# A gating unit's small product, issued three ticks instead of two behind the scaling of its rows

## The chip, the core and the metric

The kernel runs on one core of a Trainium2 chip. The metric is the device time of one execution in microseconds (us), the median of several runs. Lower is better.

The engines named here: PE (matmul; PEld is its weight load), DVE (vector), ACT (scalar, activations), POOL (GpSimd, which also issues some transfers), SP (which issues most transfers). Each works through its own queue in order and waits for others by semaphores.

## The reference, cut to what matters

One decoder layer on 512 tokens of width 2048, in float32. Of it, this case touches the spatial gating unit (gMLP):

```python
proj  = rmsnorm(x, attn_norm_g) @ w_in           # [u | v_sgu | q | k | v_att | g_a | g_b]
u     = gelu(u)
v_sgu = rmsnorm(gelu(v_sgu), sgu_norm_g)         # over each group of 128 columns
...
mixed = einsum('gts,bnsgc->bntgc', tril(w_s), v) # chunks of 128 tokens, 8 groups
y_a   = u * (mixed + b_s)
```

The rest (stick-breaking attention, two gated up-projections, w_o, SwiGLU, a gated per-layer embedding) only matters as the work that stands around it.

## The kernel before

All activations lie transposed: columns on the 128 partitions, the 512 tokens along a row. A large product is done over 256-column **units** by a seven-product (Strassen) scheme, each operand split into a high and a low part (`whi`, `wlo`) so that three fp32r matmuls stand for one fp32 matmul. For one output block of 256 columns a **Pair** runs through 8 inner units, taken two by two: four **doubles**, each with its own slot of split weights (three slots in rotation: `whi_75/wlo_76`, `whi_77/wlo_78`, `whi_79/wlo_80`). `L701` is the matmul of the five products whose right operands stand doubled, `L296` to `L298` are the three matmuls of the other two.

Weights of a double come in by two SP transfers (`L341`, `L349`) into a landing; then POOL issues a transfer that adds two further blocks onto them (`L370`); ACT makes the high parts (`L366`, five blocks, then two), DVE two more sums (`L382`) and the low parts (`L363`). ACT copies finished PSUM products out (`L757`) and DVE combines them (`L760`) during the last double of a block.

**Ticks.** While `Pair.add` writes out a double it calls `tick()` twice: after the fourth and after the seventh product, so a block of four doubles holds eight ticks. Work that stands beside the large products is written as generators; `beside(steps)` starts one a tick later, and each `yield n` asks to be continued n ticks on. So a `yield` is a place in every engine's program, not a time. The order of the PE program is the order of writing; the other engines' small instructions are placed by the framework's scheduler, with the weights' own instructions chained in their order.

**The gating unit.** The output blocks run `... s0 s1 u0 s2 u1 s3 u2 u3 ...`. A block `s` holds two groups. When it is done, DVE scales it by the row norm (`L1250`), ACT applies gelu (`L1344`; `L1348` for a `u`), and `sgu_v` starts beside the next blocks. For each of its two groups ("first half", "second half"): SP fetches the group's spatial weights (`L1222`, then masked by POOL, `L1223`) and biases (`L1226`); two ticks later PE flips the rows (`L1055`, four transposes into a bank of the two-bank pool `small`), ACT takes the squares (`L1062`, four times), DVE scales them (`L1231`), POOL raises them to -1/2 (`L954`, called the pow below); a tick later ACT scales the flipped rows (`times`, four `L1078`); some ticks later PE multiplies them with the spatial weights (`L1240`, four fp32 matmuls, each of which reads one of the four quarters that `L1078` wrote), and DVE scales the product and adds the bias (`L1241`). Then the second half begins in the same step. At `L1349` a `u` block is multiplied into the result. s0's second half and s1's first half overlap; s2 and s3 stand alone.

Both halves share one tile for the spatial weights and one for the bias, so the next `L1222` waits for `L1240`, and the next `L1226` for `L1241`.

Of the kernel before, what the change touches and what calls it, by code (L numbers as in the profile page):

```python
# [70 lines left out]
def hybrid_layer(  # L71
# [109 lines left out]
    def small_bank():  # L181
        return psa.tile([P, T], F32, tag="small", name=nm("small"))
# [769 lines left out]
    def power(ms, n):  # L952
        r = rms_tile()[:, :n]
        nc.gpsimd.tensor_tensor(out=r, in0=ms, in1=expo[:, :n], op=ALU.pow)  # L954
        return r
# [89 lines left out]
    def a_tile(tag, n=T, start=0):  # L1045
        return att[tag].f(start, start + n)
# [4 lines left out]
    def flip(o):  # L1051

        ps = small_bank()
        for t in range(NT):
            nc.tensor.transpose(ps[:, t * P : (t + 1) * P], o[:, t * P : (t + 1) * P], ident)  # L1055
        return ps

    def squares(ps):

        ms, junk = small(NT), tmp.tile([P, P], F32, tag="diag", name=nm("sq"))  # L1060
        for t in range(NT):
            nc.scalar.activation(junk, ps[:, t * P : (t + 1) * P], AF.Square,  # L1062
                                 accum_out=ms[:, t : t + 1])
        return ms
# [10 lines left out]
    def times(dst, ps, r):  # L1075
        for t in range(NT):
            s = slice(t * P, (t + 1) * P)
            nc.scalar.activation(dst[:, s], ps[:, s], AF.Copy, scale=r[:, t : t + 1])  # L1078
# [138 lines left out]
    def sgu_v(rnd, o):  # L1217

        for h in range(2):
            g = 2 * rnd + h  # L1220
            ws = a_tile("w2", P, rnd % 2 * P)
            nc.sync.dma_start(out=ws, in_=wsT[g])  # L1222
            nc.gpsimd.affine_select(out=ws, in_=ws, pattern=[[1, P]], compare_op=ALU.is_ge,  # L1223
                                    fill=0.0, base=0, channel_multiplier=-1)
            bb = a_tile("w1", P, rnd % 2 * P)
            nc.sync.dma_start(out=bb, in_=b_s[g : g + 1, :].broadcast_to([P, P]))  # L1226
            yield 2
            gv = a_tile(("l", "w0")[rnd % 2])
            ps = flip(o[:, h * T : (h + 1) * T])
            ssq = squares(ps)  # L1230
            nc.vector.tensor_scalar(out=ssq, in0=ssq, scalar1=1.0 / P, scalar2=EPS,  # L1231
                                    op0=ALU.mult, op1=ALU.add)
            rr = power(ssq, NT)
            yield 1
            times(gv, ps, rr)
            yield 2
            mp = small_bank()
            for t in range(NT):
                s = slice(t * P, (t + 1) * P)
                nc.tensor.matmul(mp[:, s], gv[:, s], ws, start=True, stop=True)  # L1240
            nc.vector.scalar_tensor_tensor(  # L1241
                out=o[:, h * T : (h + 1) * T].rearrange("p (n t) -> p n t", t=P),
                in0=mp.rearrange("p (n t) -> p n t", t=P),
                scalar=gcol[:, g_sgu + g : g_sgu + g + 1],
                in1=bb.unsqueeze(1).to_broadcast([P, NT, P]),
                op0=ALU.mult, op1=ALU.add)
# [78 lines left out]
    for n, ((w, i), pr) in enumerate(zip(order, made())):  # L1325
        if n == 0:
            row1 = norm1.row()
            for eps, c in ((eps_cols, EPS), (eps_q, EPS * P)):
                nc.vector.tensor_scalar(out=eps, in0=norm1.mean, scalar1=c, scalar2=None,
                                        op0=ALU.mult)  # L1330
        if n == 0:
            a_tiles()
        o = pr.out(block(w, i) if n < 3 else None)
        if w == "q":
            beside(q_prep(o, i))
        elif w == "k":
            kT, rk = o, rms_tile()
            beside(k_prep(kT, rk))
            beside(attention(i, kT, rk, a_tile("v", 1024)), 6)
        elif w == "v":  # L1340
            beside(v_prep(o, a_tile("v", 1024)))
        elif w == "s":
            scaled(o, row1)
            nc.scalar.activation(o, o, AF.Gelu_apprx_tanh)  # L1344
            beside(sgu_v(i, o))
        elif w == "u":
            scaled(o, row1)
            nc.scalar.activation(o, o, AF.Gelu_apprx_tanh)  # L1348
            nc.vector.tensor_tensor(out=y_a[i].f(), in0=o, in1=y_a[i].f(), op=ALU.mult)  # L1349
            y_done["a", i] = True  # L1350
        else:
            d = tc.dram_tile([P, 1024], F32, name=nm("gsp"))
            nc.sync.dma_start(out=d, in_=o)
            gate_spill[w, i] = d
# [250 lines left out]
```

## Time and profile before

| | |
|---|---|
| median of 3 runs | 2653.82 us (2651.19 to 2657.2) |
| the profiled execution's own time | 2652.22 us |
| its span | 2650.5 us |
| outside the span (difference) | 1.72 us |
| instructions | 42355 |
| stretch in which the gating unit runs | about 620 to 765 us |
| DVE busy over the span | 2255.1 us (85%) |
| ACT busy over the span | 1409.0 us (53%) |
| POOL busy over the span | 451.5 us (17%) |
| mean DMA rate | 212 GB/s |

The views used: the page's shares by engine; the waits (who waited for whom, total in us, times, longest); the chain of work that ended last, in order of time (start, duration, what); the busy time of each engine by stretch; and the timeline of single engines (start, duration, instruction, and in brackets the idle time before it and what released it). PE's instruction times are partly modelled and those of POOL are rough.

### The profile page before, as it was taken

Reading aid. Unit: us, or ns where it says so; the run is one execution under the profiler, and the core shown is the slowest. Engines: PE = TensorE matmul, PEld = TensorE weight load, DVE = VectorE, ACT = ScalarE, POOL = GpSimd, SP = SyncE. Lnnn points to the kernel's source line nnn. Section 1 sums busy time; section 2 is a strip of 40 time slices with the busy share of each in tenths; the row PEclk is TensorE's granted clock in tenths of the full one; section 3 lists DMA queues with packets and bytes.
Section 4 is the critical chain, followed back from the end, with each engine's and each line's share of the span. In section 5 each row is a group of like instructions: output and inputs, shape, how many; then the busy total and the mean of one; then the engine's idle time right before and its main releaser. Section 6 shows DMA issues by size and latency. Waiting matters only on the chain.

```text
span 2650.5 us, 42355 instructions
## 1 busy us (share of the span) xinstructions
PE 2635.0 (99%) x15202; PEld 2301.7 (87%) x15202; DVE 2255.1 (85%) x3856; ACT 1409.0 (53%) x2245; POOL 451.5 (17%) x559
## 2 busy tenths in 40 slices
PE   9999999999999999999999999999999999999999
PEld 7888888889998888888888888888888888889888
DVE  8687878787887558999888888888889989989898
ACT  7756565655554335466444444444445445455543
POOL 0222223232220001101111111111110211211010
PEclk9999999999999999999999999999999999999999
DMA  6777777677775669988888788888887989988794
GB/s 209 183 195 171 194 172 192 171 192 191 175 195 186 223 224 271 254 246 212 223 213 217 197 203 203 195 212 201 202 203 225 255 227 275 225 242 254 239 269 137
DMA packets 288130, 561.46 MB, mean 212 GB/s; under 512 B 26288, under 2 KB 133552, under 8 KB 287920
## 3 DMA queue, kind: packets, MB, share of 16 engines
q1 hardware_dynamic: 225856, 440.77, 50.6%
q0 software_dynamic: 61776, 117.47, 27.8%
q8 instruction: 119, 1.95, 0.3%
q14 instruction: 91, 0.75, 0.1%
q10 hardware_dynamic: 288, 0.52, 0.1%
HBM read 507.28 MB, written 51.38 MB: 211 GB/s over the span
## 4 chain that ended last, share of the span: by engine, by line
PE 94%; DVE 3%; ACT 1%; DMA 1%; issue 1%; SPq 0%; DVEq 0%; ACTq 0%
PE ps L701 56%; PE ps L298 9%; PE ps L297 9%; PE ps L296 9%; PE small L701 6%; DVE wlo L363 1%; PE small L1181 1%; PE small L1129 1%; PE small L1055 1%; DVE parts L287 1%; DVE wholes L534 0%; DVE wholes L382 0%; PE small L1240 0%; DMA wholes<-x 0%; DMA wholes<-w_ffn_out 0%
## 5 line engine op out<-in xcount | busy, mean ns | idle before, releaser
L701 PE MATMUL ps<-parts,whi 128*128 128x512 f32 x4390 | 1470.6, 398 | 1.9 <-DVE out L806 0.8
L366 ACT ACTIVATE whi<-wholes 128x512 fp32r<-128x512 f32 (+2 forms) x934 | 873.1, 948 | 759.4 <-DVE wholes L382 308.6
L363 DVE TENSOR_TENSOR wlo<-wholes,whi 128x512 fp32r<-128x512 f32 (+2 forms) x934 | 980.8, 1086 | 78.5 <-ACT whi L366 77.6
L701 PEld LDWEIGHTS ps<-parts,wlo 128*128 128x128 f32 x4390 | 823.9, 188 | 188.0 <-DVE wlo L363 2.5
L701 PE MATMUL ps<-parts,wlo 128*128 128x256 f32 x4390 | 868.4, 279 | 1.1 <-DVE wlo L363 1.1
L701 PEld LDWEIGHTS ps<-parts,whi 128*128 128x128 f32 x4390 | 707.2, 189 | 11.3 <-issue 3.1
L297 PE MATMUL ps<-parts,whi 128*128 128x256 f32 (+1 forms) x1622 | 538.4, 332 | 1.0 <-DVE parts L287 0.9
L298 PE MATMUL ps<-parts,wlo 128*128 128x256 f32 (+1 forms) x1622 | 538.3, 333 | 1.1 <-DVE wlo L363 1.1
L296 PE MATMUL ps<-parts,whi 128*128 128x256 f32 (+1 forms) x1612 | 532.5, 332 | 1.8 <-ACT parts L286 1.4
L382 DVE TENSOR_TENSOR wholes<-wholes 128x256 f32<-128x256 f32 x820 | 346.3, 422 | 15.8 <-DVE wlo L363 0.4
L760 DVE TENSOR_TENSOR out<-out,ps 128x256 f32<-128x256 f32 x525 | 216.8, 416 | 152.2 <-ACT out L757 152.0
L297 PEld LDWEIGHTS ps<-parts,whi 128*128 128x128 f32 x1622 | 305.9, 189 | 37.9 <-DVE parts L287 2.9
L298 PEld LDWEIGHTS ps<-parts,wlo 128*128 128x128 f32 x1622 | 306.2, 189 | 30.6 <-DVE wlo L363 1.5
L296 PEld LDWEIGHTS ps<-parts,whi 128*128 128x128 f32 x1612 | 303.5, 189 | 32.2 <-ACT parts L286 2.2
L370 POOL DMA_DIRECT2D wholes<-w_ffn_in x169 | 147.6, 873 | 704.2 <-DVE wholes L382 209.7
L370 POOL DMA_DIRECT2D wholes<-w_in x132 | 117.0, 888 | 543.1 <-DMA wholes<-w_in 112.3
L701 PE MATMUL small<-parts,whi 128*128 128x512 f32 x480 | 190.2, 397 | 0.0
L757 ACT ACTIVATE out<-ps 128x256 f32<-128x256 f32 x279 | 104.7, 385 | 57.0 <-PE ps L701 52.9
L287 DVE TENSOR_TENSOR parts<-wholes,parts 128x1024 fp32r<-128x1024 f32 (+3 forms) x139 | 124.0, 904 | 12.6 <-ACT parts L286 12.5
L286 ACT ACTIVATE parts<-wholes 128x1024 fp32r<-128x1024 f32 (+3 forms) x139 | 107.8, 797 | 46.5 <-DVE wholes L534 32.4
L370 POOL DMA_DIRECT2D wholes<-w_ffn_out x64 | 55.9, 873 | 356.0 <-DMA wholes<-w_ffn_out 84.7
L1428 ACT ACTIVATE out<-out 128x512 f32<-128x512 f32 x44 | 27.9, 633 | 156.2 <-DVE out L1427 156.2
(135 smaller groups left out, 1833.6 us busy)
## 6 DMA issues: line engine op xcount, KB each, us to landing
wholes<-w_ffn_in SPq DMA_DIRECT2D x169, 384.0 KB, 5.6
wholes<-w_in SPq DMA_DIRECT2D x132, 384.0 KB, 5.0
wholes<-w_ffn_in SPq DMA_DIRECT2D x169, 256.0 KB, 4.8
wholes<-w_ffn_in POOLq DMA_DIRECT2D x169, 256.0 KB, 5.4
wholes<-w_in SPq DMA_DIRECT2D x132, 256.0 KB, 4.1
wholes<-w_in POOLq DMA_DIRECT2D x132, 256.0 KB, 5.0
wholes<-w_ffn_out SPq DMA_DIRECT2D x64, 384.0 KB, 6.0
wholes<-x SPq DMA_DIRECT2D x46, 512.0 KB, 6.1
```

The source lines that it names most:

```text
L286: return (nc.scalar.activation(hi, src, AF.Copy), nc.vector.tensor_tensor(out=lo, in0=src, in1=hi.bitcast(F32), op=ALU.subtract))
L287: nc.vector.tensor_tensor(out=lo, in0=src, in1=hi.bitcast(F32), op=ALU.subtract))
L296: nc.tensor.matmul(ps, sh, mh, start=start, stop=False)
L297: nc.tensor.matmul(ps, sh, ml, start=False, stop=False)
L298: return nc.tensor.matmul(ps, sl, mh, start=False, stop=stop)
L363: in_turn(nc.vector.tensor_tensor(out=self.lo[:, blocks], in0=r, in1=h.bitcast(F32), op=ALU.subtract))
L366: in_turn(nc.scalar.activation(h, r, AF.Copy))
L370: nc.gpsimd.dma_start(out=raw[:, 3:5], in_=self.src[:, 1:3], accum_op=ALU.add)
L382: in_turn(nc.vector.tensor_tensor(out=o, in0=x, in1=y, op=ALU.add))
L701: m = nc.tensor.matmul(out, l, r, start=first and k == 0, stop=last and k == 1)
L757: in_turn(nc.scalar.activation(out, x, AF.Copy, scale=scale))
L760: in_turn(nc.vector.tensor_tensor(out=out, in0=x, in1=y, op=op))
```

## The change

One number. After the step that issues the scaling of the flipped rows, `sgu_v` lets three ticks go by before it issues the product, where it let two go by:

```diff
             rr = power(ssq, NT)
             yield 1
             times(gv, ps, rr)
-            yield 2
+            yield 3
             mp = small_bank()
             for t in range(NT):
                 s = slice(t * P, (t + 1) * P)
```

No instruction is added or removed. What follows in the generator moves with it: in the first half the product by one tick, and with it the second half's two transfers, mask, flip, squares, pow and scaling; the second half's product by two ticks. The scheduler places the instructions of ACT, DVE, POOL and SP anew around that.

On PE, at the first half of s0, one piece of the difference (`small` is the product's bank, the `ps` are the large product's banks; the block is s1, at the border between its third and fourth double):

```order
@@ -3173,5 +3173,4 @@
 L297 MATMUL ps_6410<-parts,whi_77 128x256
 L298 MATMUL ps_6410<-parts,wlo_78 128x256
-L1240 MATMUL small_6523<-wholes 128x128 x4
 L701 MATMUL ps_6376<-parts,whi_75 128x512
 L701 MATMUL ps_6376<-parts,wlo_76 128x256 x2
@@ -3186,4 +3185,5 @@
 L701 MATMUL ps_6397<-parts,wlo_76 128x256 x2
 L701 MATMUL ps_6397<-parts,whi_75 128x512
+L1240 MATMUL small_6559<-wholes 128x128 x4
 L701 MATMUL ps_6405<-parts,whi_75 128x512
 L701 MATMUL ps_6405<-parts,wlo_76 128x256 x2
```

The four matmuls stood between two doubles and now stand four products into the next one.

On ACT, at the second half of s2, before (the gelu `L1348` is that of u1; `sq`, `ms` are the squares, `rr` the pow's result):

```order
L366 ACTIVATE whi_75<-wholes 128x1280
L1062 ACTIVATE sq_7266,ms_7265<-small_7260 128x128 x4
L1348 ACTIVATE out_7206<-out_7206 128x1024
L366 ACTIVATE whi_75<-wholes 128x512
L366 ACTIVATE whi_79<-wholes 128x1280
L1078 ACTIVATE wholes<-small_7260,rr_7272 128x128 x4
L366 ACTIVATE whi_79<-wholes 128x512
L366 ACTIVATE whi_77<-wholes 128x1280
```

The same place now:

```order
L366 ACTIVATE whi_75<-wholes 128x1280
L1348 ACTIVATE out_7197<-out_7197 128x1024
L366 ACTIVATE whi_75<-wholes 128x512
L366 ACTIVATE whi_79<-wholes 128x1280
L1062 ACTIVATE sq_7298,ms_7297<-small_7292 128x128 x4
L366 ACTIVATE whi_79<-wholes 128x512
L366 ACTIVATE whi_77<-wholes 128x1280
L1078 ACTIVATE wholes<-small_7292,rr_7304 128x128 x4
L366 ACTIVATE whi_77<-wholes 128x512
```

The squares moved behind the gelu and two weight splits, and between them and the scaling stand two weight splits, no longer the gelu and two.

On POOL, from the first half of s1 to that of s2, before (`rr_6701` is the pow of s1's first half, `rr_6842` that of its second, `rr_7131` that of s2's first):

```order
L954 TENSOR_TENSOR rr_6701<-ms_6694,expo 128x4
L370 DMA wholes<-w_in 128x512 x2
L1223 AFFINE_SELECT wholes<-wholes 128x128
L370 DMA wholes<-w_in 128x512
L954 TENSOR_TENSOR rr_6842<-ms_6835,expo 128x4
L370 DMA wholes<-w_in 128x512
L1223 AFFINE_SELECT wholes<-wholes 128x128
L370 DMA wholes<-w_in 128x512 x4
L954 TENSOR_TENSOR rr_7131<-ms_7124,expo 128x4
```

The same place now (`rr_6695`, `rr_6874`, `rr_7131`):

```order
L954 TENSOR_TENSOR rr_6695<-ms_6688,expo 128x4
L370 DMA wholes<-w_in 128x512
L1223 AFFINE_SELECT wholes<-wholes 128x128 x2
L370 DMA wholes<-w_in 128x512 x2
L954 TENSOR_TENSOR rr_6874<-ms_6867,expo 128x4
L370 DMA wholes<-w_in 128x512 x2
L1223 AFFINE_SELECT wholes<-wholes 128x128
L370 DMA wholes<-w_in 128x512 x2
L954 TENSOR_TENSOR rr_7131<-ms_7124,expo 128x4
```

The second half's pow moved behind one more weight transfer. It is the same in s2 and s3.

## The prediction

> **What bounds the kernel now.** First the page: the shares by engine, and the chain that ended last.
>
> ```profile
> PE 2635.0 (99%) x15202; PEld 2301.7 (87%) x15202; DVE 2255.1 (85%) x3856; ACT 1409.0 (53%) x2245; POOL 451.5 (17%) x559
> PE 94%; DVE 3%; ACT 1%; DMA 1%; issue 1%; SPq 0%; DVEq 0%; ACTq 0%
> ```
>
> PE bounds the kernel; all its idle time is 2650.5 - 2635.0 = 15.5 us. The question is how much of that lies where the gating unit runs. The busy time by stretch says none (PE is the first pair after the length), and the weight load's waits between 600 and 800 us are a single line:
>
> ```profile
> 670.00:690.00 20.00, 20.00 (x133) 18.19 (x132) 17.39 (x28) 10.13 (x17) 5.68 (x6) 1.00 0.78 187
> PEld small L1240 <- ACT wholes L1078: 0.2, 1, 0.2
> ```
>
> A busy PE can hide a wait in a matmul's modelled length, so I read the chain's pieces too (start, duration; the first five from s1's second half, the last two from s3's):
>
> ```profile
> 664.83 0.43 PE small L1055 x4
> ...
> 670.20 2.81 PE ps L701 x16
> 673.01 0.89 PE small L1240 x8
> ...
> 676.03 3.50 PE ps L701 x20
> ...
> 718.19 3.50 PE ps L701 x20
> ...
> 757.37 1.18 PE small L1240 x8
> ...
> 760.68 3.50 PE ps L701 x20
> ```
>
> A product costs PE 0.89 us, in the middle of a double as here or between two, and once 1.18: 0.29 us of waiting inside the row. With the 0.2 above, the waits that this edit can remove come to about **0.5 us**, 0.02% of the time. A measurement here can tell about 0.2% (5.3 us) from no change; the three runs shown differ by 6.0 us. So a gain that can be seen is excluded, and the question is what new wait there is.
>
> **How tight the product was.** ACT and POOL at the same place:
>
> ```profile
> 669.30 1.06 ACT L1348 ACTIVATE out<-out 128x1024 f32<-128x1024 f32 x1 [2.42 <-DVE out L1250]
> 670.26 1.78 ACT L366 ACTIVATE whi<-wholes 128x512 fp32r<-128x512 f32 x2
> 671.95 1.14 ACT L1078 ACTIVATE wholes<-small,rr 128x128 f32<-128x128 f32 x4
> ...
> 675.23 1.28 ACT L366 ACTIVATE whi<-wholes 128x1280 fp32r<-128x1280 f32 x1 [0.97 <-PE ps L297]
> ...
> 756.87 1.15 ACT L1078 ACTIVATE wholes<-small,rr 128x128 f32<-128x128 f32 x4 [0.47 <-POOL rr L954]
> ...
> 669.57 0.89 POOL L370 DMA_DIRECT2D wholes<-w_in  x1 [5.05 <-DVE out L1250]
> 670.16 1.74 POOL L954 TENSOR_TENSOR rr<-ms,expo 128x4 f32<-128x4 f32 x1
> 675.74 0.92 POOL L370 DMA_DIRECT2D wholes<-w_in  x1 [3.83 <-DVE wlo L363]
> ...
> 717.82 0.95 POOL L370 DMA_DIRECT2D wholes<-w_in  x1 [3.76 <-DVE wlo L363]
> ```
>
> The scaling `L1078` ends at 673.09 while PE begins the product at 673.01: quarter by quarter, just in time, because it stands on ACT behind the gelu and two splits. PE is not held further because each matmul needs one quarter only. So the two ticks were tight, and a third looks like slack. But the squares, the pow and the scaling of each second half move too, one tick.
>
> **PE's new positions.** A product placed four products into the next double comes, in s1's second half, at 676.03 + 2.81 - 0.89 = 677.95 (its own 0.89 no longer lies ahead of it). In s2's: 718.19 + 2.81 - 0.89 = 720.11. In s3's: 760.68 + 2.81 - 1.18 = 762.31.
>
> **The three second halves: when is the scaling ready?** The squares now stand behind the gelu and two splits, from about 671.9, and take 4 x 0.40 = 1.6 us: 673.5. The 0.40 is the distance of two of them:
>
> ```profile
> 665.30 0.28 ACT L1062 ACTIVATE sq<-small 128x128 f32<-128x128 f32 x1
> ...
> 665.70 0.28 ACT L1062 ACTIVATE sq<-small 128x128 f32<-128x128 f32 x1
> ```
>
> DVE's `L1231` stands behind two `L382` that end about then; no loss. The pow is not next, though: POOL now has the `L370` of 675.74 ahead of it, whose weights SP requested at 671.07, 4.67 us before:
>
> ```profile
> 664.45 0.38 SPq L341 DMA_DIRECT2D wholes<-w_in  x1
> ...
> 671.07 0.38 SPq L341 DMA_DIRECT2D wholes<-w_in  x1
> ...
> 698.44 0.38 SPq L341 DMA_DIRECT2D wholes<-w_in  x1
> ...
> 704.21 0.88 POOL L370 DMA_DIRECT2D wholes<-w_in  x1 [3.33 <-DVE out L760]
> ```
>
> That request is released by DVE and hardly moves, so the pow can start 0.6 us behind the `L370` (670.16 - 669.57), at 676.3. How long it then takes depends on DVE:
>
> ```profile
> 653.95 1.03 POOL L954 TENSOR_TENSOR rr<-ms,expo 128x4 f32<-128x4 f32 x1
> ...
> 697.25 2.06 POOL L954 TENSOR_TENSOR rr<-ms,expo 128x4 f32<-128x4 f32 x1
> ...
> 738.44 0.89 POOL L370 DMA_DIRECT2D wholes<-w_in  x1 [4.57 <-DVE ms L1231]
> 739.00 2.43 POOL L954 TENSOR_TENSOR rr<-ms,expo 128x4 f32<-128x4 f32 x1
> ...
> 669.52 2.09 DVE L363 TENSOR_TENSOR wlo<-wholes,whi 128x1280 fp32r<-128x1280 f32 x2
> ...
> 696.92 2.09 DVE L363 TENSOR_TENSOR wlo<-wholes,whi 128x1280 fp32r<-128x1280 f32 x2
> ...
> 739.08 2.09 DVE L363 TENSOR_TENSOR wlo<-wholes,whi 128x1280 fp32r<-128x1280 f32 x2
> ```
>
> It took 1.03 us with DVE quiet. Beside a pair of low-part splits it ended 0.29 us (671.90 to 671.61), 0.30 us (699.31 to 699.01) and 0.26 us (741.43 to 741.17) behind the pair's end, wherever it had begun. In the new order DVE has, at that time:
>
> ```profile
> 632.18 1.49 DVE L363 TENSOR_TENSOR wlo<-wholes,whi 128x1280 fp32r<-128x1280 f32 x1 [0.43 <-ACT whi L366]
> ...
> 675.46 0.74 DVE L1241 SCALAR_TENSOR_TENSOR wholes<-small,gcol,wholes 128x512 f32<-128x512 f32 x1
> 676.12 0.87 DVE L382 TENSOR_TENSOR wholes<-wholes 128x256 f32<-128x256 f32 x2
> 676.91 2.18 DVE L363 TENSOR_TENSOR wlo<-wholes,whi 128x1280 fp32r<-128x1280 f32 x2
> ...
> 719.07 2.08 DVE L363 TENSOR_TENSOR wlo<-wholes,whi 128x1280 fp32r<-128x1280 f32 x2
> ...
> 761.27 2.09 DVE L363 TENSOR_TENSOR wlo<-wholes,whi 128x1280 fp32r<-128x1280 f32 x2
> ```
>
> `L1241` leaves this place (676.12 - 675.46 = 0.66 us) and `L1231` adds about 0.1, so the split of 676.91 begins at 676.35. Only its first part, 1.49 us, follows at once: the second needs an ACT split that now stands behind the scaling. DVE falls idle at 677.85, and by the rows above the pow ends 0.3 behind, at 678.15. `L1078` follows 0.05 later (671.95 behind a pow that ended at 671.90), and PE can begin about 0.50 after that (757.37 behind 756.87, where it came just in time). So 678.70 against 677.95: **PE waits about 0.75 us.** In s2, with the same step of 0.56 earlier: 719.07 - 0.56 + 1.49 + 0.30 + 0.05 + 0.50 = 720.85 against 720.11 (the `L370` of 717.82 is early enough): 0.74. In s3: 761.27 - 0.56 + 2.34 = 763.05 against 762.31: 0.74. Together 2.2 us. The later places are reckoned on the old clock, since a wait of PE moves the rest with it.
>
> Bounds of this term: nothing if the pow takes its 1.03 us (676.3 + 1.03 = 677.3, product possible at 677.9); per place 2.3 us if the `L370` comes as late as the longest pair quoted, 704.21 - 698.44 = 5.77 behind its request, and the pow ends as far behind the `L370` as the longest, 741.43 - 738.44 = 2.99: 671.07 + 5.77 + 2.99 + 0.05 + 0.50 = 680.4, 2.4 with the request where it was, 2.3 with `L1231`'s 0.1 gone ahead of it. I take the middle value, as three rows out of three show a pow that outlasts the pair.
>
> The Trainium skill (page "SBUF — State Buffer", section "Who interferes with whom") says that a DVE instruction with two SBUF inputs and a GpSimd instruction that reads SBUF lock one port pair against each other, for a whole instruction, and that the order of issue decides. The trace agrees that the two collide; but a lock per instruction would let the pow in behind the `L382` in flight, at about 676.35, to end near 677.4, and PE would not wait. The quoted rows, where the pow outlasts two instructions, speak for the longer hold, so the sum above stands and the rule's result is a rival below.
>
> **The first halves and the overlap of s0 with s1.** A first half keeps its flip, squares, pow and scaling; only its product moves, by 2.81 us, so its wait can only shrink. In the overlap s0's second scaling moves by a tick (2.1 or 2.8 us) and stands behind three squares of s1 (3 x 0.40 = 1.2 us): at most 4.0 us later. Its product moves by two ticks, a double: 676.03 - 670.20 - 0.89 = 4.94 us. No cost taken; without that cover, the price is again under 1 us.
>
> **DVE and the banks.** `L1241` of a first half moves into the combining of a finished block, 0.75 us between the fourth and fifth product's steps; but as the product no longer stands ahead of that double, the double begins 0.89 us earlier and the combining with it. Nothing net. The `L1241` that frees a bank of `small` stands more than a double ahead of the flip that takes it.
>
> **SP, POOL and the weights behind the moved waits.** `L1222` holds SP until the product is done, with weight requests queued behind:
>
> ```profile
> 659.93 0.33 SPq L1222 DMA_DIRECT2D wholes<-wsT  x1
> ```
>
> Released about 2.8 us later, at 662.8, it is still ahead of the next request's own release, 664.45 above. Splits wait on ACT behind `L1078` up to 2 us longer. They write the slot that PE has just left (the `L366` of 675.23 waited for `L297`), and with three slots PE comes back to it two doubles, some 10 us, later. Cost nil; if the cover were gone, the same 1 to 2 us at each of few places.
>
> **Sum.** -0.5 + 2.2 = +1.7 us on the profiled 2652.22 us: 2653.9. The median of the runs shown stands 1.6 us above that execution (2653.82), so I predict **2655.5 us**.
>
> **Rivals.**
> - *The extra tick simply relieves PE* (the pow slips in between DVE's instructions). For it: the 1.03 us row, and PE's slack with it. Against: the three pows above. -0.5: 2653.3 us.
> - *Slower:* the second half's pow is held by its new neighbour, the weight transfer. Place: POOL, `L370` ahead of `L954`; price 2.3 us in three places, less 0.5: +6.4, 2660.2 us. It decides from a mean wait of (5.3 + 0.5)/3 = 1.9 us on. Against it: at this place the transfer came 4.67 us after its request.
> - *A weight split comes late* because of what ACT and DVE now have ahead of it: one or two doubles wait 1 to 2 us, about +3 beside the forecast's +1.7: 2658.5 us. Against: the 10 us above.
>
> **How the numbers follow.** Forecast (waits of 0.3 to 1 us at the three places) 0.62; relieved 0.21; weight transfer 0.10; late split 0.07. Run to run the three times shown reach 3 us to either side. The range takes the relieved case less 3 and the slower rival whole: 2650.3 to 2660.5. More than 0.2% slower: half of the weight-transfer case, and 0.05 of the others by spread, 0.10. Faster: spread alone, 0.03. Within: 0.87.
>
> **What would show it.** In the profile after: `L1240` waiting on `L1078`, or rows of 1.2 us or more, in the three second halves and not in the first; `L1078` there with idle time ahead of it that `L954` ended; the wait of 0.2 gone; `L1241`'s idle time (on `L1240`) smaller. Wrong would be: PE idle on `wlo` or `whi` in 640 to 780 us, a first half that waits, or any difference after 800 us.

## The result, and the profile after

The changed kernel takes **2660.43 us** (median of 22 runs, 2654.18 to 2666.42), the kernel before, on the same chip, 2653.91 us (22 runs, 2651.19 to 2659.03). The ratio is 1.0020, with a 95% interval of 1.0013 to 1.0027 (3.5 to 7.2 us): slower, by 6.5 us between the medians and by 5.4 between the means, to which this ratio lies closer. Two more sets of runs of the same change (below) gave 1.0017 and 1.0012. The point forecast, 2655.5 us, lay 4.9 us too low. The stated range, up to 2660.5 us, holds the median by 0.07 us only, which is chance.

The execution that was profiled first took 2654.18 us, the shortest of the 22. The two profiled later (`after_again`, `after_third`) took 2660.62 and 2659.82 us and stand for the median. So three profiles of one program can be compared. The one profile of the kernel before (2652.22 us) is shorter than its median, too. The page of the first and that of `after_again`, busy time by engine:

```profile
PE 2635.2 (99%) x15202; PEld 2303.0 (87%) x15202; DVE 2255.8 (85%) x3856; ACT 1406.9 (53%) x2245; POOL 449.8 (17%) x559
```

```profile
PE 2638.9 (99%) x15202; PEld 2304.9 (87%) x15202; DVE 2254.9 (85%) x3856; ACT 1407.2 (53%) x2245; POOL 448.6 (17%) x559
```

PE's idle time is 17.3 us in the first (2652.5 - 2635.2) and 20.0 in the other (2658.9 - 2638.9), where it was 15.5. But PE's busy time also grew, by 3.9 us in `after_again`, with the same 15202 matmuls: some of them ran longer. Where, the chain of waits shows when the same piece is looked up in each trace: the double at 601 us, ahead of the gating unit, and the first whole double behind the second product of s1, of s2 and of s3. Start, duration, piece; before, then `after_again`, then `after_third`:

```profile
601.51 3.51 PE ps L701 x20
...
680.97 3.51 PE ps L701 x20
...
723.13 3.51 PE ps L701 x20
...
765.62 3.51 PE ps L701 x20
```

```profile
601.47 3.51 PE ps L701 x20
...
686.25 3.50 PE ps L701 x20
...
729.89 3.51 PE ps L701 x20
...
773.90 3.51 PE ps L701 x20
```

```profile
601.61 3.51 PE ps L701 x20
...
683.85 3.50 PE ps L701 x20
...
727.50 3.51 PE ps L701 x20
...
771.48 3.51 PE ps L701 x20
```

The differences of these starts say how much longer each stage took than before (the first profile has its pieces at 601.26, 683.21, 725.39 and 767.58):

| profile | own time | s0 and s1 | s2 | s3 | together |
|---|---|---|---|---|---|
| the first | 2654.18 | +2.49 | +0.02 | -0.30 | +2.21 |
| `after_third` | 2659.82 | +2.78 | +1.49 | +1.49 | +5.76 |
| `after_again` | 2660.62 | +5.32 | +1.48 | +1.52 | +8.32 |

The growth in the gating unit's stretch accounts for the first profile's own time against before (+1.96) and that of `after_again` (+8.40). In `after_third` (+7.60) the other 1.8 us lie behind it: between 2000 and 2640 us PE is busy for 635.6 us, where it was 637.5 before and 637.4 and 636.6 in the other two profiles. The gating unit does not stand there, and the cause stays open. What PE waits for in the gating unit's stretch, from the waits between 600 and 800 us (line, released by; us in total, times, longest), first of the first profile, then of `after_again`:

```profile
PE ps L701 <- DVE out L760: 0.7, 1, 0.7
PE ps L701 <- DVE wholes L760: 0.7, 1, 0.7
```

```profile
PE small L1240 <- ACT wholes L1078: 4.5, 3, 2.0
PE ps L701 <- DVE out L760: 0.7, 1, 0.7
```

There are two kinds. **The product waits for the scaling**, the forecast wait: three times in `after_again`, twice in `after_third`, never in the first profile. **And a large product waits for its bank**, once or twice in all three, which was forecast at nothing.

**The first wait, at s1's second half.** The chain in `after_again`:

```profile
678.01 0.86 POOL wholes L370
678.87 2.02 POOL rr L954
680.91 0.38 ACT wholes L1078
681.33 1.62 PE small L1240 x8
682.96 1.28 PE ps L701 x4
684.24 0.21 PE ps L296
```

The end is set by POOL: weight transfer, pow, scaling, product, in the order that the forecast named. The timeline of SP, POOL and PE there gives the request, the durations and what was waited for; the second line, of the view of transfers, gives the request's size and its time from issue to landing:

```profile
672.89 0.38 SPq L341 DMA_DIRECT2D wholes<-w_in  x1
wholes<-w_in SPq DMA_DIRECT2D x1, 256.0 KB, 4.4
678.01 0.86 POOL L370 DMA_DIRECT2D wholes<-w_in  x1 [5.40 <-DVE wlo L363]
678.58 2.30 POOL L954 TENSOR_TENSOR rr<-ms,expo 128x4 f32<-128x4 f32 x1
```

```profile
681.33 1.62 PE L1240 MATMUL small<-wholes 128*128 128x128 f32 x8 [2.00 <-ACT wholes L1078]
...
726.49 1.26 PE L1240 MATMUL small<-wholes 128*128 128x128 f32 x8 [1.07 <-ACT wholes L1078]
...
770.49 1.26 PE L1240 MATMUL small<-wholes 128*128 128x128 f32 x8 [1.42 <-ACT wholes L1078]
```

The bracket behind `L370` names a split of DVE. But that transfer adds onto what `L341` brings, and it follows the landing: 5.12 us behind the request here, 4.4 for the landing and 0.7 more, and by 0.6 to 0.7 at every other place given below. So it is the landing that POOL waits for.

The first halves' rows there show 1.05 to 1.13 us and no wait. A wait costs more than its brackets say: from the product's start to the next double's is 3.02 us in the first profile's s3 (764.56 to 767.58) where nothing waited, 3.40 and 3.41 behind the waits of 1.07 and 1.42 (726.49 to 729.89, 770.49 to 773.90), and 4.92 behind the wait of 2.00 (681.33 to 686.25). Short windows of `after_again` show why the last is so long (columns: PE, PEld, DVE, ACT, POOL busy with counts, then the granted clock, DMA share, GB/s):

```profile
681.50:682.00 0.50, 0.50 (x5) 0.50 (x6) 0.00 (x0) 0.50 (x4) 0.27 (x1) 1.00 1.17 213
682.00:682.50 0.50, 0.50 (x4) 0.50 (x4) 0.00 (x0) 0.50 (x2) 0.00 (x0) 0.51 1.08 232
...
684.50:685.00 0.50, 0.50 (x4) 0.50 (x4) 0.38 (x1) 0.00 (x0) 0.00 (x0) 0.50 1.03 297
685.50:686.00 0.50, 0.50 (x7) 0.50 (x6) 0.00 (x0) 0.50 (x1) 0.13 (x1) 1.00 1.02 204
```

The granted clock fell to 0.50 at 682.0 us, when PE was at work again, and stayed there for some 3.4 us. A matmul of `L296` took 0.21 us in the chain above, where it takes 0.12 elsewhere. That is 1.9 us on top of a wait of 2.0.

**The second wait, for a bank.** The chain of the first profile, in the overlap of s0 and s1:

```profile
636.26 1.08 POOL rr L954
...
637.63 0.88 ACT wholes L1078 x3
638.51 0.69 ACT whi L366
...
639.54 0.41 ACT wholes L757
...
644.10 0.75 DVE wholes L1241
644.85 0.34 DVE wholes L760
645.21 1.03 DVE wholes L760 x2
...
646.38 0.71 PE ps L701 x3
```

It starts at a pow again. ACT stood at the scaling, and behind it in its queue stood a split and the copying out of the finished products (`L757`); these came late, DVE's combining with them, and the moved `L1241` put another 0.75 us ahead of the `L760` that frees the bank. ACT's timeline in the same profile, at this place and at the one 24 us later:

```profile
637.36 1.14 ACT L1078 ACTIVATE wholes<-small,rr 128x128 f32<-128x128 f32 x4 [3.50 <-POOL rr L954]
...
661.02 1.14 ACT L1078 ACTIVATE wholes<-small,rr 128x128 f32<-128x128 f32 x4 [2.34 <-POOL rr L954]
662.04 1.29 ACT L366 ACTIVATE whi<-wholes 128x1280 fp32r<-128x1280 f32 x1
663.20 0.95 ACT L757 ACTIVATE out<-ps 128x256 f32<-128x256 f32 x3
```

The three copies run back to back from 663.20: they were ready and stood behind the scaling. These waits, too, cost more than their brackets. From the flip ahead of such a place to the next double are 2.56 us where nothing waits (651.41 to 653.97) and 3.55 behind the wait of 0.73 (645.05 to 648.60): about 1.0 us each, and the two are 2.0 of the first profile's 2.49 us in s0 and s1.

The first of the two places hangs on a landing, too, for its pow, that of s0's first half, stands behind a transfer of its own: 5.37 and 5.42 us behind the request in the first profile and in `after_third`, where the bank is late, and 4.01 in `after_again`, where it is not. The pow at the second place waits for its squares, and the bank there is late in all three.

### The profile page after: what moved, and what is told of

It reads as the page before. It is cut to its first block, busy times and chain, and to the rows that moved or that the text cites. A ratio compares the mean times of both kernels' runs of the same rounds, so it can differ in the third digit from the quotient of the medians.

```text
span 2652.5 us, 42351 instructions
## 1 busy us (share of the span) xinstructions
PE 2635.2 (99%) x15202; PEld 2303.0 (87%) x15202; DVE 2255.8 (85%) x3856; ACT 1406.9 (53%) x2245; POOL 449.8 (17%) x559
## 4 chain that ended last, share of the span: by engine, by line
PE 93%; DVE 3%; DMA 2%; ACT 1%; issue 1%; POOL 0%; SPq 0%; DVEq 0%; ACTq 0%; POOLq 0%
PE ps L701 56%; PE ps L298 9%; PE ps L297 9%; PE ps L296 9%; PE small L701 6%; DVE wlo L363 1%; PE small L1129 1%; PE small L1181 1%; PE small L1055 1%; DVE parts L287 1%; DMA wholes<-w_gate 0%; DVE wholes L534 0%; ACT whi L366 0%; DVE wholes L382 0%; DMA wholes<-x 0%
## 5 line engine op out<-in xcount | busy, mean ns | idle before, releaser
L296 PE MATMUL ps<-parts,whi 128*128 128x256 f32 (+1 forms) x1612 | 533.1, 333 | 1.9 <-ACT parts L286 1.2
L382 DVE TENSOR_TENSOR wholes<-wholes 128x256 f32<-128x256 f32 x820 | 347.3, 424 | 16.3 <-DMA wholes<-w_ffn_out 0.9
L760 DVE TENSOR_TENSOR out<-out,ps 128x256 f32<-128x256 f32 x525 | 217.2, 417 | 159.0 <-ACT out L757 158.5
L296 PEld LDWEIGHTS ps<-parts,whi 128*128 128x128 f32 x1612 | 303.9, 189 | 31.7 <-ACT parts L286 1.6
L370 POOL DMA_DIRECT2D wholes<-w_ffn_in x169 | 147.3, 872 | 705.2 <-DVE wholes L382 248.4
L370 POOL DMA_DIRECT2D wholes<-w_in x132 | 116.8, 889 | 538.8 <-DMA wholes<-w_in 138.1
L757 ACT ACTIVATE out<-ps 128x256 f32<-128x256 f32 x279 | 104.0, 383 | 54.7 <-PE ps L701 50.6
L370 POOL DMA_DIRECT2D wholes<-w_ffn_out x64 | 55.7, 871 | 354.7 <-DMA wholes<-w_ffn_out 102.7
```

The costliest lines, as they stand in the source:

```text
L296: nc.tensor.matmul(ps, sh, mh, start=start, stop=False)
L370: nc.gpsimd.dma_start(out=raw[:, 3:5], in_=self.src[:, 1:3], accum_op=ALU.add)
L382: in_turn(nc.vector.tensor_tensor(out=o, in0=x, in1=y, op=ALU.add))
L757: in_turn(nc.scalar.activation(out, x, AF.Copy, scale=scale))
L760: in_turn(nc.vector.tensor_tensor(out=out, in0=x, in1=y, op=op))
```

## The experiments

Base for all is the kernel before or after; the flip's `yield 2`, the scaling's `yield 1` and the product's `yield 2` (before) or `yield 3` (after) are the three numbers at play. `h` is 0 in a first half, 1 in a second.

| label | what | median us | its before | ratio, 95% interval |
|---|---|---|---|---|
| `after_again` | the change | 2659.28 | 2654.68 | 1.0017, 1.0009 to 1.0026 |
| `first_product` | only first halves' products later | 2655.21 | 2654.68 | 0.9997, 0.9989 to 1.0006 |
| `second_product` | only second halves' products later | 2655.27 | 2654.68 | 1.0000, 0.9991 to 1.0009 |
| `second_flip` | second halves later as a whole | 2670.18 | 2654.68 | 1.0050, 1.0036 to 1.0064 |
| `pow_first` | the change, pow ahead of the transfer | 2655.39 | 2655.32 | 1.0000, 0.9991 to 1.0009 |
| `flip_pow_first` | `second_flip`, pow ahead of the transfer | 2660.46 | 2655.32 | 1.0023, 1.0014 to 1.0032 |
| `second_late` | the change, second products a tick later still | 2656.02 | 2655.32 | 1.0001, 0.9993 to 1.0010 |
| `after_third` | the change | 2659.90 | 2655.28 | 1.0012, 1.0004 to 1.0021 |
| `two_lows` | the change, wide low-part split in two | 2657.93 | 2655.28 | 1.0010, 1.0002 to 1.0019 |

### The change taken apart

`after_again` is the changed kernel itself, beside the three that follow.

> The changed kernel once more, to see an execution that is not the fastest one. Bank theory (the first half's bias step L1241 now stands inside the combining of a finished block, so DVE gives the fifth product's bank back late and PE waits on L760 a block later): +3 to +9 us against before, PE waits on L760 at two to four of the blocks s1, u0, u1, u2, 0.7 to 2 us each. Pow theory (the second half's pow stands behind one more weight transfer, so L1240 of the second halves waits on L1078): the same +3 to +9 us, but as waits or long rows of L1240 in the second halves. Spread theory (nothing but run to run): within 2 us of before.

It confirmed the size, +4.6 us here, and gave the profile read above.

`first_product` moves only the product of the first halves, and lets nothing behind it move:

```diff
-            yield 2
+            yield 2 - h
             gv = a_tile(("l", "w0")[rnd % 2])
...
             times(gv, ps, rr)
-            yield 2
+            yield 3 - h
```

> Only the four first halves' products stand one tick later; flips and second products are where they were before. Bank theory: most of the loss is here, +2 to +7 us, with PE waits on L760. Pow theory: within 1.5 us of before, since no pow has moved behind a weight transfer. Spread theory: within 2 us.

No difference. The first half's `L1241` stands in the combining here too, at 665.37 in this profile, and PE waits for no bank there. Moving it alone costs nothing that these runs can tell; by the interval that is at most 1.6 us.

`second_product` moves only the product of the second halves:

```diff
             times(gv, ps, rr)
-            yield 2
+            yield 2 + h
```

> Only the four second halves' products stand one tick later behind an unmoved scaling; no bias step moves into a combining. Bank theory: 0 to -1 us against before (the just-in-time waits of 0.5 us are gone). Pow theory: 0 to -1 us as well, since the pow has not moved. If this one loses over 2 us, both fall.

No difference either: neither product alone is what costs. But the profile has one wait of `L1240`, 1.28 us at 638.19. That is s0's first half, which this edit does not move and which has two ticks here, as in the kernel before. Two more kernels below have two ticks there, and with them the four profiles of this one place say what sets the wait:

| profile | request to landing | request to `L370` | `L1240` waits | difference |
|---|---|---|---|---|
| before | 2.9 | 3.54 | none | |
| `flip_pow_first` | 4.1 | 4.80 | 0.90 | 3.90 |
| `second_product` | 4.5 | 5.17 | 1.28 | 3.89 |
| `second_flip` | 5.4 | 6.11 | 2.22 | 3.89 |

Each microsecond by which the transfer stands more than 3.9 us behind its request is a microsecond of waiting. The kernel before has the same two ticks there; its one profile met the shortest landing of the four. In no profile of a kernel with a third tick does the product wait there.

`second_flip` leaves the distance from scaling to product at two ticks and moves the second halves as a whole by one:

```diff
-            yield 2
+            yield 2 + h
             gv = a_tile(("l", "w0")[rnd % 2])
```

> The four second halves are moved whole by one tick (flip, squares, pow, scaling, product), the first halves' products are where they were. Bank theory: within 1.5 us of before. Pow theory: most of the loss is here, +2 to +7 us, as waits of PE on L1078 or long rows of L1240 in the second halves.

Slower by 15.5 us (6 runs; 13.4 between the means), about three times as much as the change beside it (4.6). Its profile has five waits of the product, 9.1 us in all; one is that of s0's first half, which the edit does not move, and the largest is that of s2's second half:

```profile
640.81 1.52 PE L1240 MATMUL small<-wholes 128*128 128x128 f32 x8 [2.22 <-ACT wholes L1078]
...
730.75 2.08 PE L1240 MATMUL small<-wholes 128*128 128x128 f32 x8 [3.21 <-ACT wholes L1078]
```

So most of the cost (6.9 us of the 9.1, and what follows those waits) comes with the new place of the second half's flip, squares, pow and scaling, and a third tick behind the scaling covers most of it. What in that place is late was still open: the pow's queue on POOL, its collision with DVE, or the squares on ACT.

### The pow's neighbour on POOL

`pow_first` is the changed kernel, but at the gating unit's place the transfers `L370` are written one piece later, with a dependency of order alone on the second half's pow. PE's and SP's orders are those of the changed kernel; on ACT the scaling also stands ahead of one split more.

```diff
             def landed():
                 if self.kind == "S":
-                    nc.gpsimd.dma_start(out=raw[:, 3:5], in_=self.src[:, 1:3], accum_op=ALU.add)
+                    d = nc.gpsimd.dma_start(out=raw[:, 3:5], in_=self.src[:, 1:3],
+                                            accum_op=ALU.add)
+                    if powers:
+                        tc.add_manual_dep(
+                            d.ins, powers.pop(),
+                            mybir.DependencyInfo(mybir.DependencyClass.NoSync,
+                                                 mybir.DependencyReason.DATA),
+                            reason="behind the pow")
...
                 if i in TICKS[n]:
                     tick()
+                if i == 3 and gating[0]:
+                    add_blocks()
...
-            rr = power(ssq, NT)
+            rr = rms_tile()[:, :NT]
+            d = nc.gpsimd.tensor_tensor(out=rr, in0=ssq, in1=expo[:, :NT], op=ALU.pow)
+            if h:
+                powers[:] = [d.ins.name]
```

> The changed kernel, but on POOL each second half's pow stands ahead of the weight transfer L370 that the change put before it (the transfer waits for the pow, not the other way round); PE's and SP's orders are those of the changed kernel. Queue theory (the pow waits behind that transfer's landing, and with it the scaling and the product): the loss of 4.6 to 6.5 us goes, time within 1.5 us of the kernel before, no wait of L1240 on L1078 in the second halves, the pow over before 677 us in s1's. Port theory (the pow is held by DVE's splits beside it): most of the loss stays, +3 us or more, since DVE's work is the same. Late-squares theory (gelu and two splits ahead of the squares are what makes the scaling late): the loss stays, +3 us or more.

The whole loss is gone (1.0000). POOL at s1's second half (the pow's line is 1249 in this kernel):

```profile
675.99 2.21 POOL L1249 TENSOR_TENSOR rr<-ms,expo 128x4 f32<-128x4 f32 x1 [3.73 <-DVE ms L1246]
678.28 0.92 POOL L370 DMA_DIRECT2D wholes<-w_in  x1
```

The pow begins as soon as its squares are there, 2.59 us earlier than in `after_again`. It is held by DVE no less than there (2.21 us, and as long in s2 and s3), and the squares stand where they stood; no product waits, and PE's wait for banks in the stretch is 0.3 us in all. So the queue on POOL, with a landing at its head, is the cause, not DVE alone and not the squares. That the banks are hardly late is not shown to come of the edit: a transfer still stands ahead of s0's first pow, and it came 4.26 us behind its request here.

`flip_pow_first` puts the same two edits of POOL's order on `second_flip`.

> The second halves moved whole by one tick as in second_flip (+15.5 us there), with the pow ahead of that weight transfer on POOL. Queue theory: at least two thirds of the 15.5 us go, leaving 0 to +5 us (with two ticks between scaling and product it is still tight). Port or late-squares theory: +10 us or more stay.

+5.1 us in place of +15.5 by the medians, 0.23% in place of 0.50% by the ratios: between half and two thirds of that loss were the same queue, and at least two thirds were expected. The rest is waits of the product, 5.5 us in five. Three of them, 3.8 us, stand two ticks behind a scaling whose pow still takes 2.2 us beside DVE; the other two are 0.90 at s0's first half (above) and 0.83 at its second, where the pow took 1.2 us.

`second_late` keeps the pow behind the transfer and gives the second half's product a fourth tick:

```diff
             times(gv, ps, rr)
-            yield 3
+            yield 3 + h
```

> The changed kernel with four ticks instead of three ahead of each second half's product, so that PE comes 2.1 us later to it; the pow stays behind the weight transfer. All three theories: the waits of L1240 in after_again (2.0, 1.1 and 1.4 us) shrink to at most 0.3 each and the time comes to within 2 us of the kernel before. If it stays at +4 us or more, PE's wait at the product is not what costs.

The loss is gone again (1.0001), with no wait of `L1240` on `L1078`, though the transfer came 5.44 and 5.40 us behind its request in s1 and s2. The late pow costs through the product's wait; one more tick of room hides it. Waits for banks remain, 2.8 us in five, in the profile, which is of the longest of the 11 executions; the median shows no loss from them.

### The distance of the transfer, and how DVE holds the pow

`after_third` is the changed kernel once more, to see whether its long and short executions differ at the transfer.

> The changed kernel once more, for a third profile of it. In its two profiles so far the weight transfer L370 ahead of the second half's pow came 3.58, 4.12 and 3.63 us behind its request L341 in the execution of 2654.18 us (no wait of L1240 there) and 5.12, 5.26 and 6.15 us in the one of 2660.62 us (waits of 2.00, 1.07 and 1.42). Queue theory: the same program's time follows these distances. With the pow ending 0.9 us behind a wide low-part split that is in flight, a place with under 4.2 us between L341 and L370 shows no wait of L1240 on L1078, one with over 5 us shows a wait of 0.8 to 2.2; a profiled execution of 2658 us or more has at least two such places, one under 2656 has none. Median 2658 to 2661. Rival (the spread of the times comes from elsewhere, the distances go with it by chance): a slow execution without such waits, or such waits in a fast one.

They do. From the request `L341` to the `L370` that adds onto what landed, us, and the product's wait:

| profile | s1 | s2 | s3 |
|---|---|---|---|
| the first | 3.58, none | 4.12, none | 3.63, none |
| `after_third` | 3.54, none | 5.39, 1.07 | 5.17, 1.40 |
| `after_again` | 5.12, 2.00 | 5.26, 1.07 | 6.15, 1.42 |

Up to 4.12 us no place waited; from 5.12 on each did. In every one of the nine the transfer stands 0.6 to 0.7 us behind the landing of its request, which took 2.9 to 5.5 us for the same 256 KB. DVE's timelines at the nine places show what the distance decides besides the pow's start: where it was short, the pow met a short instruction (a second split of 0.7 us or an `L382` of 0.4), where it was long the next weights' wide split of 1.49 us. So the landing decides first of all; why the same load lands after 2.9 us in one execution and after 4.4 in another was not found.

`two_lows` splits the wide low-part instruction, so as to see what the pow is held by:

```diff
-                split(True, slice(0, c), raw)
+                for b in (slice(0, 2), slice(2, c)) if gating[0] and c == 5 else (slice(0, c),): split(True, b, raw[:, b])
```

> The changed kernel, with the wide low-part split L363 (128x1280, 1.49 us) written as two instructions of 128x512 and 128x768 (0.68 and about 0.92 us) while the gating unit runs; the values are the same and every other engine keeps its order. What is disputed is how DVE holds the pow. Per instruction: the pow gets its turn when the DVE instruction in flight ends, and ends 0.90 behind it, so that it never lasts over 0.92 + 0.90 = 1.82 us; rows of 2.0 to 2.4 us, of which each profile so far had one to three, are gone, and the pow ends 0.9 us behind the first of the two parts where it began in that one. Held as long as DVE goes on without a pause (the forecast's reading): the ends stay where they are, 0.9 us behind the last of the two parts or later, rows of over 2 us remain. Time: DVE has room, so by the first the waits of L1240 shrink by up to 0.9 us a place, and the median stands 0 to 3 us under that of the changed kernel, not under the kernel before; by the second no difference between the two.

POOL, then DVE, in s2's first half, s2's second and s3's second (the DVE rows each without what stands between them):

```profile
698.12 1.60 POOL L954 TENSOR_TENSOR rr<-ms,expo 128x4 f32<-128x4 f32 x1
...
719.83 1.41 POOL L954 TENSOR_TENSOR rr<-ms,expo 128x4 f32<-128x4 f32 x1
...
762.92 2.15 POOL L954 TENSOR_TENSOR rr<-ms,expo 128x4 f32<-128x4 f32 x1
```

```profile
698.13 0.72 DVE L363 TENSOR_TENSOR wlo<-wholes,whi 128x512 fp32r<-128x512 f32 x1
698.78 0.95 DVE L363 TENSOR_TENSOR wlo<-wholes,whi 128x768 fp32r<-128x768 f32 x1
...
719.65 0.68 DVE L363 TENSOR_TENSOR wlo<-wholes,whi 128x512 fp32r<-128x512 f32 x1
720.25 0.95 DVE L363 TENSOR_TENSOR wlo<-wholes,whi 128x768 fp32r<-128x768 f32 x1
...
762.64 0.68 DVE L363 TENSOR_TENSOR wlo<-wholes,whi 128x512 fp32r<-128x512 f32 x1
763.25 0.95 DVE L363 TENSOR_TENSOR wlo<-wholes,whi 128x768 fp32r<-128x768 f32 x1
```

The first pow ends at 699.72, 0.87 us behind the first part's end (698.85), while DVE goes on with the second and a third. The next ends at 721.24, 0.91 behind the first part (720.33). DVE going on does not hold the pow: it waits for one instruction and takes 0.9 us from there. The last ends at 765.07, 0.87 behind the second part (764.20), though it began during the first: what counts is which part has begun some 0.3 us after the pow did (the second parts began 0.66, 0.42 and 0.33 us behind the three pows, and only the last of them went first). So the bound of 1.82 us in the expectation was too low and one row of over 2 us remains, but the reading that it tested holds. The time, 2.0 us under `after_third` beside it, is not told apart from it: the two intervals overlap.

None of these kernels beats the kernel before by an amount that can be measured.

## Why the prediction was right or wrong

**Place and order: right.** "POOL now has the `L370` of 675.74 ahead of it", and "PE waits about 0.75 us" in the second halves of s1, s2 and s3. The waits stand exactly there and `pow_first` shows the cause. The sign was right: slower. But whether a place waits is decided by the landing, which the forecast took as fixed: the late transfer was its rival with a chance of 0.10.

**The size of that term: wrong.** Forecast 0.74 us a place, 2.2 together; measured 2.00, 1.07 and 1.42 in `after_again` (4.5), none, 1.07 and 1.40 in `after_third` (2.5), and nothing in the first profile, the shortest of its 22 runs. The mean of the nine, 0.77, meets the forecast by luck and hides that no place waits 0.74: it is nothing or 1 to 2 us. Three things were mis-sized.

- *The pow's end.* "DVE falls idle at 677.85, and by the rows above the pow ends 0.3 behind." The three rows behind that 0.3 all had a pair of splits, of 1.49 and 0.60 us. They can be read as 0.3 behind the pair or as 0.9 behind its first instruction, and the sum took the first for a place where it had itself found that the second split does not follow. There 0.9 applies, which would make 1.34 us a place, 4.0 in three. The weighing of the Trainium skill's rule (page "SBUF — State Buffer", section "Who interferes with whom"), a lock for a whole instruction, went the wrong way for the same reason: `two_lows` agrees with the rule. It does not save the wait, as the rival by that rule had it, where the instruction that counts is the wide split: in all five places that waited it was, in the four others a short one.
- *The transfer's distance.* The sum took the one distance at this place, 4.67 us. The three profiles have 3.54 to 6.15, and with over 5 the wait is there. That is what the two slower profiles have and the shortest has not; the times of the changed kernel spread over 12.2 us, those of before over 7.8. The bound was quoted (5.77) and then left to a rival. "That request ... hardly moves" holds within 0.5 us against PE: in the first profile s1's stands at 673.72, 2.65 us later than before, and the product 2.2 us later than reckoned.
- *What follows a wait.* No price was set. It is 0.4 us behind the waits of 1.07 and 1.42, and 1.9 behind that of 2.00, where the clock fell to 0.50.

**"DVE and the banks. Nothing net": wrong,** 0.7 us of waiting once or twice in each profile, about 1.0 us of time each. The argument was that combining begins earlier with its double. It does not where ACT's copies stand behind a scaling that waits for the pow. "Splits wait on ACT behind `L1078` up to 2 us longer ... Cost nil" thought of splits alone, and "The first halves and the overlap ... No cost taken" of products alone; what stood behind the same `L1078` and had no room were the copies. `first_product` shows that the moved `L1241` alone makes no bank late; that the held scaling is the other half is read from the chain and from `pow_first`, where 0.3 us remains, and was not tried by itself.

**The waits removed, 0.5 us: right for the profiled execution.** The weight load's 0.2 is gone, and s3 of the first profile, in which nothing waits, is 0.30 us shorter than before (the 0.29 inside the row). But that execution had the shortest landing at s0's first half. With the landings of other profiles the two ticks there cost 0.9 to 2.2 us, which the third tick removes as well; how often the kernel before meets them was not measured.

**SP and the weights: right.** No product waits for `whi` or `wlo` in the stretch, so the rival of a late split is out.

**The rivals.** "Relieved" is what the shortest execution shows at the three places, and the other two profiles do not. "Slower" named the place, the order on POOL and a total (2660.2) within 0.3 us of the median, but its price was 2.3 us in each of three places; measured were at most 2.00 and as few as none, and the rest of the time is banks and clock. That its total fits is luck as well. With the terms as the three profiles have them on average, the waits (7.0 / 3 = 2.3), what follows them (four of 0.4 and one of 1.9, 3.5 / 3 = 1.2) and the banks (five of 1.0, 1.7), less 0.5, make +4.7 us in the stretch, where the table above has +5.4 on average; that is a sum made afterwards, not a test.

## What to carry to other kernels

A tick added ahead of one instruction moves everything that its generator issues later: list for each moved instruction its new neighbour in its own queue, and suspect most a small one that now stands behind a transfer which waits for a landing, and then what stands behind *it* on the next engine. Slack belongs in front of the consumer without moving its producers (`second_product` and `second_late` cost nothing that can be measured, `second_flip` 15.5 us). A duration that comes from a landing is a range and not a number: here 2.9 to 5.5 us at the same few places, and one profile shows one draw of it. And when a rule is read off rows of one kind (a pair of splits), check that the place it is used for has that kind.

## What the runs showed of the hardware that was not expected

The granted clock fell to 0.50 for some 3.4 us behind a single PE wait of 2.00 us, and as long behind the waits of 2.22 and 3.21 in `second_flip`. Behind waits of 1.07 and 1.42 the next double came only 0.4 us late, and behind one of 1.64 in `second_flip` the clock stayed at 1.00; where the limit lies between that and 2.00, if it is a limit of the wait's length alone, was not tried.

A pow of 128x4 elements on POOL takes 1.03 to 1.4 us where no two-operand DVE instruction holds it, and otherwise ends about 0.9 us behind the one that is in flight some 0.3 us after the pow's start (0.87 to 0.91 in `two_lows`, 0.87 to 0.91 at the nine places of the changed kernel).

A transfer that POOL issues onto what a load of 256 KB brings stands 0.6 to 0.7 us behind that load's landing, at all 13 places given above, whether the landing took 2.9 us or 5.5.
